# Splits in the down projections in another order: input, next sums, raw pieces; fewer fast pairs, and weight sums kept out of the output projections

## The chip, the cores and the metric

One Trainium2 chip, one core of it. The metric is the device time of one execution in microseconds (us), the median of the runs. Less is better.

## What is computed

A trunk of two encoder layers over 256 tokens of width 2048, all in float32. Each layer has an attention sub-layer (differential attention in layer 0, windowed grouped attention in layer 1, and four heads into a memory of 256 tokens), an output projection, and an MLP. The change lies in the MLP and in what is done ahead for it:

```python
for i in range(DEPTH):                       # DEPTH = 2
    h = rms_norm(x, norm_attn[i])
    ...
    x = x + heads @ w_out[i]
    h = rms_norm(x, norm_mlp[i])
    x = x + jnp.square(jax.nn.relu(h @ w_up[i])) @ w_down[i]
```

`w_up[i]` is 2048 x 8192 and `w_down[i]` 8192 x 2048, so the two MLPs hold most of the weights, and every weight is read from memory once.

## The kernel before

**Products.** A float32 product is made of three matmuls in a faster format: each operand is split into `hi`, its rounded copy, and `lo`, what the rounding left out, and hi·hi + hi·lo + lo·hi are summed (`three`, L512 to L515). `split` (L420 to L422) makes the two parts: ScalarE (ACT) casts the copy in L421, VectorE (DVE) subtracts in L422. Weights and inputs both pass through it.

**Pieces and pairs.** Weights come in pieces of 128x1024 (512 KB), in the order of `plan`. `fetch` (L361) loads and splits a piece; `piece` (L399) hands one out and keeps two more (AHEAD) fetched. Two pieces are a pair: four 128x512 blocks of weights and two of input, 24 matmuls of 128x512. An up projection has eight chunks `q` of eight pairs, a down projection two halves of 32 pairs.

**Fast pairs.** In some pairs seven block products do the work of eight (`seven`, L530): 21 matmuls in place of 24. They need sums of weight blocks: `a`, two blocks, and `b`, two more, each split like a piece (`sum_pair`, L340, with the additions of `b` in L348 and L349), and differences of the input. `load_pair` (L320) loads what the sums need, up to two pairs ahead (LOOK) if at least four of the buffers in `slots` are free. FAST, LATE, UP_FAST and OUT_FAST list the fast pairs.

**Sums made in memory.** For down projections `a` is made by the DMA queue of GpSimd (POOL) long before: `make_sums` (L283) copies a piece to `madesum` (L289), and adds blocks of the next one to it in a DMA that accumulates (L293). SUM_AT, SUM_GAP and SUM_GAP_UP say after which pieces; each copy waits for the split of a piece that has just been fetched (`after_piece`).

**Hidden blocks.** The relu and square of an up chunk (`to_hidden`, L992, on ACT in L1002 and L1003) leave 16 blocks `c` of hidden values, two pairs' input in each. Those of AWAY go to memory (`hid`, L1006) and come back (L359) into one of six `t2k` buffers, which also take half pieces of fast pairs (L333). The differences of the input of fast pairs are made once (`keep`, L977), stored (`kept`, L982) and read again when needed (L1094), all of it on POOL's queue. `h2_of` (L1050) splits the input of one pair of a down projection; it is called after both pieces of that pair are handed out, by when the next pair's are fetched.

**Order.** Each engine works through its instructions in order. A scheduler sorts them from the order of the code, by what each one needs; SP's queue issues the loads, POOL's the sums in memory, the `hid` and `kept` transfers. Buffers bound how far ahead things go: four each of raw pieces, `hi` and `lo`, eight of tag `x2` (the splits of the sums, `x` in the tables of order), six of `h2` (inputs and differences, `h`), ten of `blk`, and six slots in `big`.

Of the kernel before, what the change touches and what calls it, by code (L numbers as in the profile page):

```python
# [22 lines left out]
P = 128  # L23
S = 256
# [10 lines left out]
UP_FAST = (2, 4, 6)  # L35
# [34 lines left out]
def trunk(ctx: ExitStack, tc: tile.TileContext, xin, xtok, memin, memtok, posrel, gcol, rows,  # L70
# [167 lines left out]
    def fast_pairs(name, h):  # L238

        if name.startswith("out"):  # L240
            return OUT_FAST[h]
        if name.startswith("up"):
            return UP_FAST
        if name.startswith("down"):
            return LATE if (name, h) == ("down0", 1) else FAST
        return ()
# [16 lines left out]
    slots = deque()  # L263

# [18 lines left out]
    def make_sums(layer):  # L283

        name = f"down{layer}"

        def copy(h, j):
            made_in[name, h, j] = dp.tile([P, 2, 512], F32, name=nm("madesum"))
            after_piece(nc.gpsimd.dma_start(made_in[name, h, j].rearrange("p a n -> p (a n)"), weights[name][h, 2 * j]))  # L289

        def add(h, j):
            upper = weights[name][h, 2 * j + 1][:, 512:1024]
            nc.gpsimd.dma_start(made_in[name, h, j], upper.unsqueeze(1).broadcast_to([P, 2, 512]), accum_op=ALU.add)  # L293

        def after_piece(ins):
            tc.add_manual_dep(ins.ins, done[0].ins.name, mybir.DependencyInfo(mybir.DependencyClass.Sync, mybir.DependencyReason.DATA),
                              reason="behind a piece")
# [12 lines left out]

    making = deque()
    fetched = [0]
    before_up = [i for i, (name, c, j) in enumerate(plan) if name.startswith("up") and (c, j) == (0, 0)]
# [4 lines left out]
    loaded = {}  # L318

    def load_pair(name, c, p, early=False):  # L320
# [19 lines left out]
    def sum_pair(name, c, p):  # L340

        key = (name, c, p)
        first, raw, a, taken = loaded.pop(key)
        if a is None:
# [3 lines left out]
        nc.vector.tensor_tensor(b[:, 0, :], a[:, 1, :], first[:, 0:512], op=ALU.add)  # L348
        nc.vector.tensor_tensor(b[:, 1, :], b[:, 0, :], raw[:, 0:512], op=ALU.add)  # L349
# [4 lines left out]
        slots.extend(taken)  # L354
# [6 lines left out]
    def fetch(parts=1, lead=None):  # L361
# [6 lines left out]
        if seven_:  # L368
            load_pair(name, c, p)
            raw = loaded[name, c, p][j % 2]  # L370
        else:
            raw = wp.tile([P, 1024], F32, tag="raw", name=nm("raw"))
# [10 lines left out]
        if seven_:  # L383
            with tc.issue_after(done[0].ins):
                if j % 2 == 1:
                    split(hi[:, 0:512], lo[:, 0:512], raw[:, 0:512])
                    sum_pair(name, c, p)
                else:
                    split(hi, lo, raw)
        else:  # L390
            for i in range(parts):
# [4 lines left out]
                done[0] = split(hi[:, s], lo[:, s], raw[:, s])  # L396
        ready.append(((name, c, j), hi, lo))
# [132 lines left out]
    def seven(own, side, first_, last_, two, sums2, at, t2):  # L530
# [11 lines left out]
        three(side[2], first_, last_, d(2), (bh, bl), LOWER)  # L542
        three(own[0][1], False, False, lambda part: at(1, 1, part), (bh, bl), UPPER)
# [422 lines left out]
    def mlp(layer, X2, last):  # L966
# [4 lines left out]
        slots.extend(wide[:, i] for i in range(4))  # L971
# [38 lines left out]
        for q in range(8):  # L1010
            tag, other = ("mm", "aux") if q % 2 == 0 else ("aux", "mm")
            own = [[bank(tag) for _ in range(2)] for _ in range(2)]
            for j in range(8):
                if j == UP_FAST[0]:
                    side = [bank(other) for _ in range(4)]
                if q == 0 and j + 1 in UP_FAST:
                    diffs[j + 1] = quad("h2" if j + 1 == UP_FAST[0] else "blk", (P, 2, 512))
                    pair_differences(X2.pairs[j + 1], diffs[j + 1])
# [5 lines left out]

                if j in UP_FAST:
                    seven(own, side, j == UP_FAST[0], j == UP_FAST[-1], two, sums.pop((name, q, j)), at, diffs[j])
# [10 lines left out]
                if j == UP_FAST[-1]:  # L1037
# [7 lines left out]
        slots.extend(blk([P, 4, S], F32) for _ in range(2))  # L1045
# [9 lines left out]
        for half_ in range(2):  # L1055
# [219 lines left out]
```

## Time and profile before

| | |
|---|---|
| time, median of 3 runs | 2109.35 us (2105.58 to 2110.53) |
| the profiled execution | 2104.56 us |
| its span in the trace | 2102.8 us |
| TensorE (PE) busy | 2079.2 us, 99% |
| VectorE (DVE) busy | 1781.1 us, 85% |
| ScalarE (ACT) busy | 1278.5 us, 61% |
| read and written in memory | 532.76 MB and 94.50 MB, 298 GB/s |

In us from the span's start, the up projection of layer 0 runs from about 417 to 768, its down projection to 1105; layer 1 has them at about 1410 to 1759 and to 2102. The second halves of the down projections begin at about 950 and 1929.

A row of the timeline gives start, duration, engine, line, operation, the tiles written and read, the number of equal instructions in a row, and in brackets how long the engine stood idle before and what ended that. Durations of matmuls overlap, since they are pipelined: their starts tell the rate. A row of the windows gives the length of the stretch, PE's busy time and the number of its matmuls with a record, the granted clock, the busy share of the DMA engines and GB/s. A row of the waits reads: who, on which line, waits for whom: us in all, times, longest.

### The profile page before, as it was taken

The page shows a single profiled execution, that of the slowest core. Times are in us where ns is not written, and L with a number is a line of the kernel's source. Part 1 is how long each engine was busy: PE and PEld are TensorE (multiplying, and loading weights), DVE is VectorE, ACT ScalarE, POOL GpSimd, SP SyncE. Part 2 cuts the span into 40 slices and gives each one's busy share as a digit, 9 for nine tenths or more (in the row PEclk, how much of TensorE's full clock was granted, in tenths as well). Part 3 has the DMA queues.
Part 4 walks back from the last instruction along what each step waited for, and adds up shares of the span by engine and source line. Part 5 has one row for each costly group of instructions (what it writes and reads, how often), then busy time and mean ns, then how long its engine had stood idle before and what let it go on. Part 6 is the DMA issues. An engine that isn't in the chain of part 4 may idle for free.

```text
span 2102.8 us, 28801 instructions
## 1 busy us (share of the span) xinstructions
PE 2079.2 (99%) x9999; PEld 1719.7 (82%) x9999; DVE 1781.1 (85%) x2571; ACT 1278.5 (61%) x1902; POOL 185.1 (9%) x290
## 2 busy tenths in 40 slices
PE   9999999999999999999999999999999999999999
PEld 8888888788888888788888888888888887878877
DVE  7677778898999898898877677889999888888887
ACT  7467665565665666667555566556665656666664
POOL 1200000100010100000000100010001110000000
PEclk9999999999999999999999999999999999999999
DMA  9788877877887789978968878787888899998894
GB/s 320 262 270 262 264 239 215 255 233 235 254 296 249 251 312 307 329 259 283 326 248 262 248 226 251 216 252 230 266 262 264 282 305 320 305 330 291 298 326 151
DMA packets 168002, 565.21 MB, mean 269 GB/s; under 512 B 19424, under 2 KB 20448, under 8 KB 166624
## 3 DMA queue, kind: packets, MB, share of 16 engines
q1 hardware_dynamic: 131680, 438.05, 59.5%
q0 software_dynamic: 36032, 125.32, 22.3%
q8 instruction: 78, 1.28, 0.2%
q14 instruction: 68, 0.56, 0.1%
q10 hardware_dynamic: 144, 0.01, 0.0%
HBM read 532.76 MB, written 94.50 MB: 298 GB/s over the span
## 4 chain that ended last, share of the span: by engine, by line
PE 71%; issue 11%; DMA 9%; DVE 6%; ACT 2%; POOL 1%; SPq 0%; ACTq 0%; DVEq 0%; POOLq 0%
PE mm L515 9%; PE mm L514 9%; PE mm L513 9%; PE aux L514 8%; PE aux L515 8%; PE aux L513 8%; PE mm L474 5%; PE mm L475 5%; PE mm L476 5%; DMA madesum<-in_w_down 4%; DVE lo L422 3%; DMA big<-in_w_up 1%; DVE x L422 1%; DMA kept<-h 1%; DMA t2k<-hid 1%
## 5 line engine op out<-in xcount | busy, mean ns | idle before, releaser
L422 DVE TENSOR_TENSOR lo<-raw,hi 128x1024 fp32r<-128x1024 f32 (+1 forms) x514 | 607.7, 1206 | 175.2 <-ACT hi L421 174.1
L421 ACT CAST hi<-raw 128x1024 fp32r<-128x1024 f32 (+1 forms) x514 | 517.0, 1036 | 371.2 <-PE mm L476 119.5
L474 PE MATMUL mm<-hi,x 128*128 128x512 f32 x640 | 256.5, 403 | 1.9 <-ACT x L417 1.9
L475 PE MATMUL mm<-lo,x 128*128 128x512 f32 x640 | 251.0, 392 | 0.1
L476 PE MATMUL mm<-hi,x 128*128 128x512 f32 x640 | 250.1, 391 | 0.0
L421 ACT CAST h<-big 128x1024 fp32r<-128x1024 f32 (+1 forms) x112 | 110.3, 993 | 119.1 <-DVE big L281 93.6
L513 PE MATMUL mm<-hi,h 128*128 128x512 f32 (+1 forms) x451 | 176.5, 392 | 3.8 <-ACT h L421 3.8
L515 PE MATMUL mm<-hi,h 128*128 128x512 f32 (+1 forms) x451 | 175.5, 394 | 4.9 <-DVE h L422 4.8
L514 PE MATMUL mm<-lo,h 128*128 128x512 f32 (+1 forms) x451 | 176.6, 392 | 0.3 <-DVE lo L422 0.2
L515 PE MATMUL aux<-hi,h 128*128 128x512 f32 x444 | 172.7, 390 | 4.0 <-DVE h L422 3.9
L514 PE MATMUL aux<-lo,h 128*128 128x512 f32 x444 | 172.9, 389 | 0.7 <-DVE lo L422 0.7
L513 PE MATMUL aux<-hi,h 128*128 128x512 f32 x444 | 173.0, 390 | 0.0
L421 ACT CAST hi<-big 128x1024 fp32r<-128x1024 f32 (+1 forms) x136 | 120.3, 899 | 63.6 <-DMA big<-in_w_up 29.0
L513 PE MATMUL aux<-hi,x 128*128 128x512 f32 x400 | 156.3, 391 | 0.0
L514 PE MATMUL aux<-lo,x 128*128 128x512 f32 x400 | 155.8, 389 | 0.0
L514 PE MATMUL mm<-lo,x 128*128 128x512 f32 x400 | 155.4, 389 | 0.0
L515 PE MATMUL mm<-hi,x 128*128 128x512 f32 x400 | 155.4, 389 | 0.0
L515 PE MATMUL aux<-hi,x 128*128 128x512 f32 x400 | 155.4, 389 | 0.0
L513 PE MATMUL mm<-hi,x 128*128 128x512 f32 x400 | 155.2, 391 | 0.0
L422 DVE TENSOR_TENSOR lo<-big,hi 128x1024 fp32r<-128x1024 f32 (+1 forms) x136 | 137.8, 1031 | 13.7 <-ACT hi L421 13.5
L474 PEld LDWEIGHTS mm<-hi,x 128*128 128x128 f32 x640 | 120.6, 189 | 26.0 <-ACT x L417 2.2
L476 PEld LDWEIGHTS mm<-hi,x 128*128 128x128 f32 x640 | 120.3, 188 | 25.9
(314 smaller groups left out, 4256.2 us busy)
## 6 DMA issues: line engine op xcount, KB each, us to landing
raw<-in_w_up SPq DMA_DIRECT2D x160, 512.0 KB, 5.3
raw<-in_w_down SPq DMA_DIRECT2D x134, 512.0 KB, 4.8
madesum<-in_w_down POOLq DMA_DIRECT2D x122, 512.0 KB, 6.2
big<-in_w_up SPq DMA_DIRECT2D x96, 512.0 KB, 4.8
raw<-in_w_a SPq DMA_DIRECT2D x72, 512.0 KB, 5.3
h<-kept POOLq DMA_DIRECT2D x61, 512.0 KB, 6.3
raw<-in_w_out SPq DMA_DIRECT2D x52, 512.0 KB, 5.4
raw<-in_w_b SPq DMA_DIRECT2D x48, 512.0 KB, 5.2
```

What stands on the lines that cost most here:

```text
L421: nc.scalar.copy(hi, src)
L422: return nc.vector.tensor_tensor(lo, src, as32(hi), op=ALU.subtract)
L474: nc.tensor.matmul(ps[t], lhsT=xh, rhs=hi[:, ws], start=(k == 0), stop=False)
L475: nc.tensor.matmul(ps[t], lhsT=xh, rhs=lo[:, ws], start=False, stop=False)
L476: nc.tensor.matmul(ps[t], lhsT=xl, rhs=hi[:, ws], start=False, stop=(k == KT - 1))
L513: nc.tensor.matmul(acc_, lhsT=x(0), rhs=w2[0][:, ws], start=first_, stop=False)
L514: nc.tensor.matmul(acc_, lhsT=x(0), rhs=w2[1][:, ws], start=False, stop=False)
L515: nc.tensor.matmul(acc_, lhsT=x(1), rhs=w2[0][:, ws], start=False, stop=last_)
```

## The change

1. The lists: FAST has 15 pairs for 16, every second one and 29, where before it had neighbours (10 and 11, 15 and 16, 20 and 21); LATE, for the second half of layer 0's down projection, has 14 for 13. The first up chunk of each layer has two fast pairs for three. Pair 2 is no longer among them, and the differences for 4, 6 and 2 are made at pairs 3, 5 and 7 (DIFF_UP).
2. In a down projection the sums of a pair are made ahead of its raw pieces, and the input of pair j + 1 is split between the two pieces of pair j. Slots go back one piece later (`held_slots`).
3. In up projections `b` is written over the raw piece that it is made from, so a pair takes three slots for four; five slots are there from the start, and early loads start when two are free.
4. The copies of `make_sums` wait for the oldest of the last four splits in place of the latest. They come every fourth piece before the memory projection, every eighth from the first piece of up on, and none begins between.
5. Hidden block 14 goes away too, so only 15 of the late ones stays in `big`.

```diff
-UP_FAST = (2, 4, 6)
+UP_FAST = ((4, 6),) + ((2, 4, 6),) * 7
+DIFF_UP = {3: 4, 5: 6, 7: 2}
-FAST = (2, 4, 6, 8, 10, 11, 13, 15, 16, 18, 20, 21, 23, 25, 27, 29)
-LATE = (2, 4, 6, 8, 10, 13, 15, 18, 20, 23, 25, 27, 29)
-AWAY = range(6, 14)
-LATE_BLK = (10, 15, 20, 25, 29)
+FAST = (2, 4, 6, 8, 10, 12, 14, 16, 18, 20, 22, 24, 26, 28, 29)
+LATE = (2, 4, 6, 8, 10, 12, 14, 16, 18, 20, 22, 24, 26, 28)
+AWAY = range(6, 15)
+LATE_BLK = (8, 12, 16, 20, 24, 28)
-SUM_AT = {0: 26, 1: 2}
-SUM_GAP = 5
-SUM_GAP_UP = 10
+SUM_AT = {0: 20, 1: 2}
+SUM_GAP = 4
+SUM_GAP_UP = 8
...
         def after_piece(ins):
-            tc.add_manual_dep(ins.ins, done[0].ins.name, ...
+            tc.add_manual_dep(ins.ins, splits[0], ...
...
-        at = fetched[0] + SUM_AT[layer]
+        first, quiet, up = [at_piece[k, layer] for k in ("in", "mem", "up")]
+        at = first + SUM_AT[layer]
         for i in range(len(wanted) + 1):
             making.append((at, lambda i=i: step(i)))
-            at += SUM_GAP if at < before_up[layer] else SUM_GAP_UP
+            at += SUM_GAP if at < quiet else SUM_GAP_UP
+            at = max(at, up) if at >= quiet else at
...
+    splits = deque(maxlen=AHEAD + 2)
...
-        if key in loaded or p not in fast_pairs(name, c) or early and len(slots) < 4:
+        if key in loaded or key in taken_raw or p not in fast_pairs(name, c) or early and len(slots) < (2 if name.startswith("up") else 4):
...
-        b = raw_quad(name, (P, 2, 512), taken)
-        nc.vector.tensor_tensor(b[:, 0, :], a[:, 1, :], first[:, 0:512], op=ALU.add)
-        nc.vector.tensor_tensor(b[:, 1, :], b[:, 0, :], raw[:, 0:512], op=ALU.add)
+        b = raw.rearrange("p (a n) -> p a n", a=2) if up else raw_quad(name, (P, 2, 512), taken)
+        nc.vector.tensor_tensor(b[:, 1, :], a[:, 1, :], first[:, 0:512], op=ALU.add)
+        nc.vector.tensor_tensor(b[:, 0, :], b[:, 1, :], raw[:, 0:512], op=ALU.add)
...
             with tc.issue_after(done[0].ins):
-                if j % 2 == 1:
+                if j % 2 == 0:
+                    if down:
+                        taken = sum_pair(name, c, p)
+                    split(hi, lo, raw)
+                else:
                     split(hi[:, 0:512], lo[:, 0:512], raw[:, 0:512])
-                    sum_pair(name, c, p)
-                else:
-                    split(hi, lo, raw)
+                    if not down:
+                        taken = sum_pair(name, c, p)
+                    slots.extend(held_slots.pop(name, []) if down else taken)
+                if down and j % 2 == 0:
+                    held_slots[name] = taken
...
-            hT.append(wide[:, c - 10] if c >= 14 else blk([P, 4, S], F32))
+            hT.append(wide[:, 5] if c == 15 else blk([P, 4, S], F32))
...
+            ats = deque([h2_of(0)])
             for j in range(32):
...
-                two = [piece(f"down{layer}", half_, 2 * j + i) for i in range(2)]
-                at = h2_of(j)
+                two = [piece(f"down{layer}", half_, 2 * j)]
+                if j < 31:
+                    ats.append(h2_of(j + 1))
+                two.append(piece(f"down{layer}", half_, 2 * j + 1))
+                at = ats.popleft()
```

What the scheduler makes of it, first in the middle of layer 1's first down half. DVE before: `lo<-raw` are the raw pieces of plain pair 17, L348 to the second `x` are the sums of pair 18 with its own pieces (`lo`) between them, and the `h` are the inputs of pairs 17, 18 and 19.

```order
L422 TENSOR_TENSOR lo_17573<-raw_17569,hi_17572 128x1024
L422 TENSOR_TENSOR lo_17579<-raw_17577,hi_17578 128x1024
L348 TENSOR_TENSOR big_13687<-big_13687,blk_16803 128x512
L422 TENSOR_TENSOR x_17626<-big_13687,x_17625 128x1024
L422 TENSOR_TENSOR lo_17616<-blk_16803,hi_17615 128x1024
L422 TENSOR_TENSOR lo_17620<-t2k_17521,hi_17619 128x512
L349 TENSOR_TENSOR big_13687<-big_13687,t2k_17521 128x512
L422 TENSOR_TENSOR h_17633<-t2k_17523,h_17633 128x512
L422 TENSOR_TENSOR h_17678<-t2k_17570,h_17678 128x512
L422 TENSOR_TENSOR x_17628<-big_13687,x_17627 128x1024
L422 TENSOR_TENSOR h_17724<-t2k_17613,h_17724 128x512
```

DVE after, a little earlier in the same half (L440 is now the subtraction of `split`, L357 and L358 the sums of `b`): inputs of pairs 14 and 15, raw pieces of 13, sums and pieces of 14, inputs of 16 and 17, raw pieces of 15.

```order
L440 TENSOR_TENSOR h_17421<-t2k_17362,h_17421 128x512
L440 TENSOR_TENSOR h_17460<-t2k_17405,h_17460 128x512
L440 TENSOR_TENSOR lo_17365<-raw_17361,hi_17364 128x1024
L440 TENSOR_TENSOR lo_17374<-raw_17372,hi_17373 128x1024
L357 TENSOR_TENSOR big_13666<-big_13666 128x512
L440 TENSOR_TENSOR x_17412<-big_13666,x_17411 128x1024
L358 TENSOR_TENSOR big_13666<-big_13666,t2k_17312 128x512
L440 TENSOR_TENSOR lo_17408<-big_13666,hi_17407 128x1024
L440 TENSOR_TENSOR lo_17425<-t2k_17312,hi_17424 128x512
L440 TENSOR_TENSOR x_17414<-big_13666,x_17413 128x1024
L440 TENSOR_TENSOR h_17512<-t2k_17453,h_17512 128x512
L440 TENSOR_TENSOR h_17551<-t2k_17496,h_17551 128x512
```

A pair's input, which stood behind that pair's raw pieces and behind the sums of the next one, now stands ahead of its raw pieces, two pairs earlier; the sums stand ahead of the pieces of their own pair.

The second place is the start of layer 1's down projection. ACT before: raw pieces of pair 0, a sum of pair 2 (`x`), raw pieces of pair 1, an input for differences, the input of pair 0 (`h_16822`), and the relu and square of hidden blocks 14 and 15.

```order
L421 CAST hi_16764<-raw_16759 128x1024
L421 CAST hi_16770<-raw_16769 128x1024
L421 CAST x_16891<-big_13687 128x1024
L421 CAST hi_16811<-raw_16810 128x1024
L421 CAST hi_16817<-raw_16816 128x1024
L421 CAST h_16750<-t2k_16751 128x512
L421 CAST h_16822<-blk_14135 128x512
L1002 ACTIVATE big_13687<-aux_16849 128x512
L1002 ACTIVATE big_13687<-aux_16856 128x512
L1003 ACTIVATE big_13687<-big_13687 128x512 x2
```

ACT after, from the input of pair 0 (`h_16776`) on: raw pieces of the last up pair, the copy for the up chunk's side sums, raw pieces of pair 0, inputs of pairs 1 and 2, raw pieces of pair 1, the first piece and a sum of pair 2, then relu and square of block 14 (L1020, L1021).

```order
L439 CAST h_16776<-blk_14108 128x512
L439 CAST hi_16678<-raw_16677 128x1024
L439 CAST hi_16684<-raw_16683 128x1024
L566 COPY t2k_16710<-mm_16507 128x512
L439 CAST hi_16725<-raw_16720 128x1024
L439 CAST hi_16731<-raw_16730 128x1024
L439 CAST h_16785<-blk_14108 128x512
L439 CAST h_16869<-blk_14123 128x512
L439 CAST hi_16780<-raw_16779 128x1024
L439 CAST hi_16789<-raw_16788 128x1024
L439 CAST hi_16855<-big_13666 128x1024
L439 CAST x_16861<-big_13666 128x1024
```

The input of pair 0 moves from behind pair 1's raw pieces to ahead of the last pieces of up. PE now also runs pair 0 ahead of the transposes of blocks 14 and 15, which stood before it.

The third is POOL's queue at the same start. Before, from the last sum in memory on (L289, L293) to the first `kept` reads (L1094):

```order
L982 DMA kept_16581<-h_16574 128x1024
L289 DMA madesum_16635<-in_w_down 16x8192
L293 DMA madesum_16635<-in_w_down 256x1x512
L982 DMA kept_16757<-h_16750 128x1024
L1094 DMA h_16945<-kept_14335 128x1024
```

After (L291 and L295 make the sums, L1024 stores `hid`, L1118 reads `kept`):

```order
L1000 DMA kept_16632<-h_16625 128x1024
L291 DMA madesum_16737<-in_w_down 16x8192
L291 DMA madesum_16769<-in_w_down 16x8192
L295 DMA madesum_16737<-in_w_down 256x1x512
L295 DMA madesum_16769<-in_w_down 256x1x512
L1024 DMA hid_16826<-blk_16818 128x512
L1024 DMA hid_16835<-blk_16818 128x512
L1118 DMA h_16928<-kept_14308 128x1024
L1000 DMA kept_16907<-h_16900 128x1024
```

The first `kept` read, which came behind a `kept` store, now comes behind one more sum and the two `hid` stores of block 14. Over the whole program PE has 12 instructions more (10,066 for 10,054 rows) and DVE 26 fewer (2488 for 2514).

More of the change, by code (lines that the diff above doesn't have):

```diff
@@ L396, in fetch @@
                 done[0] = split(hi[:, s], lo[:, s], raw[:, s])
+                splits.append(done[0].ins.name)
         ready.append(((name, c, j), hi, lo))
@@ L541, in seven @@
         three(side[3], first_, last_, d(1), (ah, al), LOWER)
-        three(side[2], first_, last_, d(2), (bh, bl), LOWER)
-        three(own[0][1], False, False, lambda part: at(1, 1, part), (bh, bl), UPPER)
+        three(side[2], first_, last_, d(2), (bh, bl), UPPER)
+        three(own[0][1], False, False, lambda part: at(1, 1, part), (bh, bl), LOWER)
     def side_sums(side):
@@ L970, in mlp @@
         slots.clear()
-        slots.extend(wide[:, i] for i in range(4))
+        slots.extend(wide[:, i] for i in range(5))
         hidden_in.clear()
@@ L1023, in at @@
                     return pair[:, kk, part, t * P:(t + 1) * P]
-                if j in UP_FAST:
-                    seven(own, side, j == UP_FAST[0], j == UP_FAST[-1], two, sums.pop((name, q, j)), at, diffs[j])
+                if j in fast:
+                    seven(own, side, j == fast[0], j == fast[-1], two, sums.pop((name, q, j)), at, diffs[j])
                 elif j < 7:
@@ L1044, in mlp @@
             Task([lambda q=q, u=u, n=n, i=i, tag=tag: to_hidden(q, n, u, i, tag) for n in range(2) for i in range(2)], wait=1, gap=0)
-        slots.extend(blk([P, 4, S], F32) for _ in range(2))
+        slots.append(blk([P, 4, S], F32))
         N2 = Halves()
```

29 lines of the change are left out of this document (19 added, 10 removed).

## The prediction, made before the result was known

> **What bounds the kernel now.** I read the page's first table, then who TensorE (PE) waits for, then PE's busy time by stretches, and only then the places where it stands still.
>
> ```profile
> span 2102.8 us, 28801 instructions
> PE 2079.2 (99%) x9999; PEld 1719.7 (82%) x9999; DVE 1781.1 (85%) x2571; ACT 1278.5 (61%) x1902; POOL 185.1 (9%) x290
> ```
>
> PE is busy for 2079.2 of 2102.8 us, so 23.6 us of it are idle. All that a new order can win is this idle time and whatever PE does slowly after it. The waits of PE (us in total, times, longest):
>
> ```profile
> PE mm L515 <- DVE h L422: 4.8, 2, 2.5
> PE mm L513 <- ACT h L421: 4.0, 3, 3.2
> PE aux L515 <- DVE h L422: 3.9, 2, 2.2
> PE mm L474 <- ACT x L417: 1.9, 1, 1.9
> ```
>
> Three of the four largest name `h` in L421 or L422: the split of a pair's input in the down projections, by ACT (hi) and DVE (lo). L422's four waits come to 8.7 us. Now stretches of 50 us: busy PE and its matmuls, granted clock, DMA share, GB/s.
>
> ```profile
> 750.00:800.00 50.00, 49.41 (x226) 1.00 0.91 330
> 800.00:850.00 50.00, 49.69 (x217) 1.00 0.90 301
> 850.00:900.00 50.00, 47.47 (x203) 0.97 0.93 330
> ...
> 950.00:1000.00 50.00, 50.00 (x222) 1.00 0.81 276
> ...
> 1750.00:1800.00 50.00, 46.40 (x207) 0.97 0.96 333
> ...
> 1850.00:1900.00 50.00, 47.71 (x203) 0.97 0.88 314
> ...
> 2000.00:2050.00 50.00, 46.05 (x202) 1.00 0.92 322
> ```
>
> The undisturbed stretch at 950 sets the price of one 128x512 matmul: 50 us / 222 = 0.225 us. Against it the stretches at 800, 850, 1850 and 2000 lack 5 + 19 + 19 + 20 = 63 matmuls, 14.2 us. Their idle time alone is 0.31 + 2.53 + 2.29 + 3.95 = 9.1 us; most of the rest is slow matmuls after a stall, and some may be records the trace lost. PE at two of the stalls:
>
> ```profile
> 1853.43 1.22 PE L515 MATMUL mm<-hi,h 128*128 128x512 f32 x2 [2.27 <-DVE h L422]
> 1854.45 0.63 PE L514 MATMUL mm<-lo,h 128*128 128x512 f32 x1
> 1854.87 0.63 PE L515 MATMUL mm<-hi,h 128*128 128x512 f32 x1
> ...
> 2021.40 0.73 PE L515 MATMUL aux<-hi,h 128*128 128x512 f32 x2 [2.25 <-DVE h L422]
> 2021.98 0.39 PE L514 MATMUL aux<-lo,h 128*128 128x512 f32 x1
> ```
>
> After 2.27 us of idling the next matmuls start 0.42 us apart, at half speed, for eight of them (some 1.6 us); after 2.25 us at 2021 they run on at full speed. The Trainium skill ("TensorE: Matmul & The Clock Gate", "Why this matters for your kernels") asks for no idle gap over about 3 us; by it a gap of 2.27 us would carry no surcharge, and the trace differs: this one did. By that rule the stalls that may vanish are worth the 9.1 us, not the 14.2.
>
> Why `h` is late, on DVE before the stall at 1853:
>
> ```profile
> 1832.08 0.69 DVE L422 TENSOR_TENSOR h<-t2k,h 128x512 fp32r<-128x512 f32 x1 [4.09 <-ACT h L421]
> 1833.04 2.36 DVE L422 TENSOR_TENSOR lo<-raw,hi 128x1024 fp32r<-128x1024 f32 x2 [0.26 <-ACT hi L421]
> ...
> 1848.61 0.69 DVE L348 TENSOR_TENSOR big<-big,blk 128x512 f32<-128x512 f32 x1
> 1849.21 1.22 DVE L422 TENSOR_TENSOR x<-big,x 128x1024 fp32r<-128x1024 f32 x1
> 1850.35 1.22 DVE L422 TENSOR_TENSOR lo<-blk,hi 128x1024 fp32r<-128x1024 f32 x1
> ...
> 1852.08 0.69 DVE L349 TENSOR_TENSOR big<-big,t2k 128x512 f32<-128x512 f32 x1
> 1852.69 1.29 DVE L422 TENSOR_TENSOR h<-t2k,h 128x512 fp32r<-128x512 f32 x2
> ```
>
> DVE stands 4.09 us at 1828, and from 1833.04 works without a break until the missing `h` at 1852.69. PE waits there for the input of pair 17, a plain pair whose own two raw pieces had long been split; ahead of its input stand the sums of pair 18. The starts in these rows give a 128x1024 step at 1.13 us and a 128x512 one at 0.60. A fast pair thus costs DVE two sums (1.2), their two splits (2.3), one and a half raw pieces (1.7) and the input (0.6), 5.8 us, against 21 matmuls or 4.7 us of PE; a plain pair costs 2.9 against 24 or 5.4. Pairs 10 to 18 of FAST before hold six fast and three plain: 43.5 of DVE to 44.4 of PE. There is no slack to catch up 4.09 us.
>
> **The change part by part.**
>
> *Order and even spacing (A).* With pairs fast in turn, two pairs cost DVE 8.7 of PE's 10.1 us, so a delay is worked off at 1.4 us in each two pairs; and the inputs of pairs 14 and 15 now stand ahead of the sums of 14 and the raw pieces of 15. All four waits of L515 are of this one kind. They are worth 9.1 us (idle alone) to 14.2 (all that is lacking). I take 13, near the upper end, since slow matmuls after a stall are seen. What is late next: the raw pieces. They are due at a pair's first matmul, but can't start before PE frees their hi and lo buffers at the end of the pair before the last, which leaves the full 4.7 to 5.4 us of a pair for about 3 us of casts and subtractions.
>
> *Start of a down projection (B).* The rows are ACT's, PE's, then POOL's, and the DMA table of 765 to 790 us:
>
> ```profile
> 1758.33 1.04 ACT L421 CAST hi<-raw 128x1024 fp32r<-128x1024 f32 x1 [3.79 <-DMA raw<-in_w_down]
> ...
> 1761.07 0.61 ACT L421 CAST h<-blk 128x512 fp32r<-128x512 f32 x1
> 1761.59 1.08 ACT L1002 ACTIVATE big<-aux 128x512 f32<-128x512 f32 x2
> 1762.55 1.15 ACT L1003 ACTIVATE big<-big 128x512 f32<-128x512 f32 x2
> ```
> ```profile
> 1756.00 1.14 PE L1000 MATMUL aux<-ident,t2k 128*128 128x128 f32 x9
> 1757.55 0.98 PE L1000 MATMUL aux<-ident,t2k 128*128 128x128 f32 x7 [0.40 <-DVE t2k L990]
> 1761.73 0.80 PE L513 MATMUL mm<-hi,h 128*128 128x512 f32 x1 [3.20 <-ACT h L421]
> ```
> ```profile
> 1762.73 0.57 POOL L1094 DMA_DIRECT2D h<-kept  x1
> ```
> ```profile
> h<-kept POOLq DMA_DIRECT2D x3, 512.0 KB, 8.3
> ```
> ```profile
> h<-kept POOLq DMA_DIRECT2D x61, 512.0 KB, 6.3
> ```
>
> Before, the input of pair 0 stands on ACT behind both raw pieces of pair 1, which land late; PE waits 0.40 and 3.20 us, and the 1750 stretch holds 191 large matmuls (43.0 us) and 16 transposes (2.1): 4.9 us are lacking. In layer 0 it is at most the 0.8 us that L513's other two waits leave of their 4.0. Now that input comes early, and pair 0 runs at once, ahead of the transposes of the last hidden blocks: 5.7 us saved. But the first `kept` read, for pair 2, now stands on POOL behind two `hid` stores of hidden block 14, and those wait for its relu and square. If pair 0 starts at T, its matmuls end at T + 5.4; ACT has one cast of pair 2 and one more ahead (2 us), then L1002 and L1003 on two tiles each (2.1 us); two stores on POOL take 1.1: the read goes out near T + 10.5. At 6.3 us (median of all) to 8.3 (median of this stretch) it lands at T + 16.8 to 18.8. PE wants it after pair 0 (5.4), the transposes (2.1), pair 1 (5.4) and twelve matmuls (2.7), T + 15.6. The new stall is 1.2 to 3.2 us in each layer, with half-speed matmuls up to 4.8; the lower end is nearer to the page's median, the upper to the crowded stretch. I take 2 each, 4 in all; B is then -1.7, with bounds -3.3 and +3.9.
>
> *Output projections and the first up chunk (C).*
>
> ```profile
> 400.00:450.00 50.00, 48.21 (x215) 1.00 0.70 211
> 450.00:500.00 50.00, 49.05 (x223) 1.00 0.77 246
> ...
> 1390.00:1440.00 50.00, 49.43 (x223) 1.00 0.73 210
> ```
>
> The sum transfers leave the stretch from the memory projection to the first up chunk, pair 2 of that chunk is fast no longer, and its differences spread over three pairs. The stretches lack 1.79 + 0.57 us, and the wait of L474 above, in the second memory projection, is 1.9: 4.3 us. The bounds are 0 and 4.3; I take 3, as each has a sum transfer or pair 2's sums beside it.
>
> *Fewer fast pairs (D).* Two in down, two in up: four pairs with 24 matmuls for 21, 12 x 0.225 = +2.7 us, all on PE.
>
> *Sum transfers closer together in up (E).* They move from every tenth piece to every eighth, in step with two `kept` stores a chunk. Stretch 450 to 500, with 0.95 us idle, is what such a meeting costs: from 0 to 14 times 0.95 = 13 us for the up chunks but the first of each layer. I take 1.5, near the lower end, as one meeting in five shows in the trace so far. Block 14's `hid` stores and reloads lie on queues beside PE, at nothing, as long as DMA has room: the share is 0.96 at most.
>
> The sum: -13 - 1.7 - 3 + 2.7 + 1.5 = -13.5 us. The profiled execution takes 2104.56 us (1.8 beyond its span), so 2091.1; it lies 4.8 below the median of the runs, 2109.35, from which the forecast is **2095.9**.
>
> **Rivals.** What a measurement of this kernel can tell from no change is about 0.3%, 6.3 us.
>
> 1. *Slower: the early input waits for its reload.* For blocks 6 to 14 the input comes from memory, and in the new order it stands ahead of sums and raw pieces on ACT and DVE, so a late reload holds everything.
>
> ```profile
>   ACT h L421: 25.8, 8
> DMA to landing us min/median/max: 2.6/5.7/10.6
> ```
>
> Those are the waits for the 64 reloads before: eight, 3.2 us each. Read from SP's order after the change, the reload for pair 15 takes the buffer that the input of pair 12 leaves, one turn of two pairs, 10.1 us, before its own use. The median of 5.7 lands in time, the maximum of 10.6 doesn't. 18 pairs a half, four halves, make 36 turns; at 0.38 us a turn the 13.5 us are gone, at 0.75 us (27 us) the result is 13.5 us slower, 2122.9. Against it: each turn can work off 1.4 us.
>
> 2. *No change: the stalls move.* Half of A returns at raw pieces (-6.5), B is at +3.9, C at -1: with D and E +0.6, 2110. For it speaks the DMA share of 0.88 to 0.96 in every disturbed stretch.
>
> 3. *No change: E at its upper end.* -13.5 - 1.5 + 13 = -2, 2107. Against it: up has DVE and DMA to spare (0.77).
>
> 4. *More.* A and C whole, B at -3.3, E nothing: -14.2 - 4.3 - 3.3 + 2.7 = -19.1, 2090.2. The runs of before reach 3.8 us below their median (2105.58 to 2109.35), which puts the lower edge near 2087.
>
> That the change isn't made by the scheduler is excluded: the order shows it.
>
> **How the numbers follow.** Forecast (8 to 18 us less) 0.55, rival 4 0.12, rival 2 0.14, rival 3 0.08, rival 1 0.11. Faster by over 0.3% (below 2103.0) are the forecast, rival 4 and 0.02 of the third: 0.69. Within 0.3%: 0.20. Slower: 0.11. The range goes from rival 4's 2087 to 2110, where rivals 2 and 3 lie; outside are rival 1 and a few strays.
>
> **What would show it.** Right: no wait of L515's counterpart for `h` over 1 us; 222 matmuls in all 50-us stretches of both down projections past their first; no wait at the first matmul of down, but one for `kept` of 1 to 3 us at pair 2; 12 more matmuls; quiet out projections. Wrong: ACT's waits for `hid` above 25.8 us with PE idle behind them; PE waiting for `lo<-raw` at the heads of pairs; stalls in every up chunk beside the sum transfers; an unchanged 14 us lacking in down.

## The result, and the profile after

The changed kernel takes 2086.76 us (median of 4 runs, 2086.09 to 2087.77), the kernel before 2108.05 (its three runs and one more, 2105.58 to 2110.53). The ratio is 0.9899, with a 95% interval of 0.9882 to 0.9917: 21.3 us less. The forecast was 2095.9, and the measured median lies 0.2 us below 2087, the lower end of its range. The profiled executions are closer together: 2104.56 and 2087.19, 17.4 us apart.

The page's head, then who PE waits for, in the changed kernel:

```profile
span 2085.4 us, 28771 instructions
PE 2073.3 (99%) x10011; PEld 1721.3 (83%) x10011; DVE 1771.0 (85%) x2545; ACT 1275.6 (61%) x1892; POOL 182.8 (9%) x286
```
```profile
PE mm L531 <- DMA h<-kept: 5.0, 2, 2.6
...
PE mm L532 <- DVE lo L440: 0.8, 1, 0.8
```

PE's idle time fell from 23.6 to 12.1 us. Of the four lines shown of before none is left: PE no longer waits for an `h` that ACT or DVE splits (8.7 us in L515 and 4.0 in L513 before), nor 1.9 us in L474. The list is headed by a wait that wasn't there, for the `kept` read.

PE in the stretches shown of before, and two more (the last is of 60 us):

```profile
750.00:800.00 50.00, 47.38 (x216) 1.00 0.92 323
800.00:850.00 50.00, 50.00 (x222) 1.00 0.90 311
850.00:900.00 50.00, 50.00 (x223) 1.00 0.97 329
...
1750.00:1800.00 50.00, 46.67 (x201) 0.93 0.97 329
...
1850.00:1900.00 50.00, 50.00 (x222) 1.00 0.91 318
...
2000.00:2050.00 50.00, 50.00 (x222) 1.00 0.96 333
```
```profile
400.00:450.00 50.00, 50.00 (x230) 1.00 0.70 216
450.00:500.00 50.00, 50.00 (x231) 1.00 0.82 262
1230.00:1290.00 60.00, 59.84 (x310) 1.00 0.64 213
...
1390.00:1440.00 50.00, 50.00 (x230) 1.00 0.76 238
```

The inside of both down projections is full: 222 or 223 matmuls in each of these stretches, with a DMA share up to 0.97. Only their first stretches got worse, 216 for 226 and 201 for 207. The head of up went from 215, 223 and 223 matmuls to 230, 231 and 230.

The wait for `kept` in layer 1: POOL's two `hid` stores and the read behind them, then PE's first matmul of the down projection, and its first with that tile.

```profile
1755.24 1.16 POOL L1024 DMA_DIRECT2D hid<-blk  x2 [8.99 <-ACT blk L1021]
1756.39 0.56 POOL L1118 DMA_DIRECT2D h<-kept  x1
```
```profile
1745.23 0.39 PE L531 MATMUL mm<-hi,h 128*128 128x512 f32 x1
```
```profile
1764.58 0.79 PE L531 MATMUL mm<-hi,h 128*128 128x512 f32 x1 [2.57 <-DMA h<-kept]
1765.17 0.63 PE L532 MATMUL mm<-lo,h 128*128 128x512 f32 x1
```

The down projection starts at 1745.23 with no wait; call that moment T. POOL waits 8.99 us for the square of block 14 (L1021) and issues the read at T + 11.2; PE gets it at T + 19.3 and had stood for 2.57 us.

The reloads of hidden blocks, on which the slower rival hung: who waited, and the time to landing (those of L368 alone, without the `hid` stores).

```profile
  ACT h L439: 1.3, 3
...
DMA to landing us min/median/max: 3.4/5.5/11.1
```

Three waits and 1.3 us for 72 reloads, where before it was eight and 25.8 us for 64, though the slowest took longer than before (11.1 us for 7.7).

### The profile page after: what moved, and what is told of

Same layout as the page of the kernel before. It is cut to its first block, busy times and chain, and to the rows that moved or that the text cites. A ratio compares the mean times of both kernels' runs of the same rounds, so it can differ in the third digit from the quotient of the medians.

```text
span 2085.4 us, 28771 instructions
## 1 busy us (share of the span) xinstructions
PE 2073.3 (99%) x10011; PEld 1721.3 (83%) x10011; DVE 1771.0 (85%) x2545; ACT 1275.6 (61%) x1892; POOL 182.8 (9%) x286
## 4 chain that ended last, share of the span: by engine, by line
PE 95%; DMA 2%; DVE 1%; issue 1%; ACT 1%; POOL 0%; SPq 0%; ACTq 0%; DVEq 0%; POOLq 0%
PE mm L531 12%; PE mm L532 12%; PE mm L533 12%; PE aux L532 11%; PE aux L533 11%; PE aux L531 11%; PE mm L492 7%; PE mm L493 7%; PE mm L494 7%; DMA h<-kept 1%; PE mm L1018 1%; PE aux L635 1%; DVE lo L440 1%; PE aux L612 1%; PE aux L654 1%
## 5 line engine op out<-in xcount | busy, mean ns | idle before, releaser
L439 ACT CAST hi<-raw 128x1024 fp32r<-128x1024 f32 (+1 forms) x522 | 525.4, 1036 | 451.1 <-issue 143.4
L440 DVE TENSOR_TENSOR lo<-raw,hi 128x1024 fp32r<-128x1024 f32 (+1 forms) x522 | 617.4, 1207 | 196.1 <-ACT hi L439 194.1
L492 PE MATMUL mm<-hi,x 128*128 128x512 f32 x640 | 256.0, 402 | 0.2 <-ACT hi L439 0.2
L493 PE MATMUL mm<-lo,x 128*128 128x512 f32 x640 | 251.0, 392 | 0.2 <-DVE lo L440 0.2
L494 PE MATMUL mm<-hi,x 128*128 128x512 f32 x640 | 250.3, 391 | 0.2 <-DVE x L436 0.2
L439 ACT CAST h<-big 128x1024 fp32r<-128x1024 f32 (+1 forms) x100 | 101.7, 1020 | 151.6 <-DVE big L283 129.6
L531 PE MATMUL mm<-hi,h 128*128 128x512 f32 (+1 forms) x461 | 179.8, 390 | 5.2 <-DMA h<-kept 5.0
L533 PE MATMUL mm<-hi,h 128*128 128x512 f32 (+1 forms) x461 | 178.9, 388 | 0.0
L531 PE MATMUL mm<-hi,x 128*128 128x512 f32 x414 | 161.8, 391 | 0.0
L533 PE MATMUL mm<-hi,x 128*128 128x512 f32 x414 | 161.1, 389 | 0.0
L532 PE MATMUL mm<-lo,x 128*128 128x512 f32 x414 | 161.1, 389 | 0.0
L440 DVE TENSOR_TENSOR lo<-big,hi 128x1024 fp32r<-128x1024 f32 (+1 forms) x141 | 144.4, 1044 | 0.2 <-ACT hi L439 0.2
L493 PEld LDWEIGHTS mm<-lo,x 128*128 128x128 f32 x640 | 120.5, 188 | 23.7 <-DVE lo L440 1.8
```

The lines of the kernel that those rows point to most:

```text
L439: nc.scalar.copy(hi, src)
L440: return nc.vector.tensor_tensor(lo, src, as32(hi), op=ALU.subtract)
L492: nc.tensor.matmul(ps[t], lhsT=xh, rhs=hi[:, ws], start=(k == 0), stop=False)
L493: nc.tensor.matmul(ps[t], lhsT=xh, rhs=lo[:, ws], start=False, stop=False)
L494: nc.tensor.matmul(ps[t], lhsT=xl, rhs=hi[:, ws], start=False, stop=(k == KT - 1))
L531: nc.tensor.matmul(acc_, lhsT=x(0), rhs=w2[0][:, ws], start=first_, stop=False)
```

## The experiments

Ratios are to the kernel before, run on the same chip in the same job. There were four jobs, each on a chip of its own; the kernel before took 2104.2, 2104.4, 2103.7 and 2102.7 us in them, single runs from 2098.7 to 2113.3. So times of two jobs can be compared by their ratios only, and the changed kernel itself ran in the second job alone.

### Which part of the reorder removed the waits for h

First the new lists with the old order of splits in the down projections. The edit undoes both moves:

```diff
                 if j % 2 == 0:
-                    if down:
-                        taken = sum_pair(name, c, p)
                     split(hi, lo, raw)
                 else:
                     split(hi[:, 0:512], lo[:, 0:512], raw[:, 0:512])
-                    ...
+                    slots.extend(sum_pair(name, c, p))
...
-                two = [piece(f"down{layer}", half_, 2 * j)]
-                ...
-                at = ats.popleft()
+                two = [piece(f"down{layer}", half_, 2 * j + i) for i in range(2)]
+                at = h2_of(j)
```

> The changed kernel with the old order of splits in the down projections (raw pieces, then sums, then the input of a pair after both its pieces); lists of fast pairs and times of the sums in memory stay new. Changed kernel: 2086.8 us. Theory 'order': PE's waits for h in L515's place return, 8 to 14 us: 2095 to 2101. Rival 'even spacing': with every second pair fast DVE works a delay off, no wait for h over 1 us: 2085 to 2090.

Measured: 2094.70 us, ratio 0.9948 (0.9930 to 0.9965). The time is about that of theory 'order', but not its reason. PE's largest wait, and ACT's in layer 0's second half (950 to 1105 us):

```profile
PE aux L526 <- DVE lo L434: 5.2, 12, 0.8
```
```profile
ACT blk L433 <- DMA big<-madesum: 18.2, 4, 5.1
```

No wait for `h` came back. Instead PE waits twelve times for `lo`, all in that half, while ACT stands 18.2 us for sums that have not been loaded into `big` (and some more for those in `blk`). Two rows of ACT's timeline there show what is queued behind such a sum:

```profile
1001.16 1.05 ACT L433 CAST blk<-blk 128x1024 fp32r<-128x1024 f32 x1 [5.04 <-DMA blk<-madesum]
1002.12 1.99 ACT L433 CAST hi<-raw 128x1024 fp32r<-128x1024 f32 x2
```

The raw pieces of a plain pair wait behind a late load for the sums of the next fast one. The three stretches from 950 to 1100 lack 42 matmuls against the changed kernel, 9.5 us; the four that lacked 63 before are full (222 each). So the rival was right about `h`, and a wait took its place that neither had named.

Then the new lists alone, in the kernel before:

```diff
-FAST = (2, 4, 6, 8, 10, 11, 13, 15, 16, 18, 20, 21, 23, 25, 27, 29)
-LATE = (2, 4, 6, 8, 10, 13, 15, 18, 20, 23, 25, 27, 29)
+FAST = (2, 4, 6, 8, 10, 12, 14, 16, 18, 20, 22, 24, 26, 28, 29)
+LATE = (2, 4, 6, 8, 10, 12, 14, 16, 18, 20, 22, 24, 26, 28)
...
-LATE_BLK = (10, 15, 20, 25, 29)
+LATE_BLK = (8, 12, 16, 20, 24, 28)
```

> The kernel before with the new lists of fast pairs of the down projections alone (FAST, LATE and where the sums' splits of LATE go). Two fast pairs fewer are +1.4 us. Theory 'order': the four waits of L515 for h stay (8.7 us of waiting), 2107 to 2111. Rival 'even spacing': the waits go, 14 us less: 2094 to 2097.

Measured: 2105.84 us, ratio 1.0004 (0.9990 to 1.0019).

```profile
PE aux L514 <- DVE lo L422: 5.0, 12, 0.8
PE mm L513 <- DMA h<-kept: 2.5, 2, 1.5
PE mm L515 <- DVE h L422: 2.1, 2, 1.1
```
```profile
850.00:900.00 50.00, 50.00 (x222) 1.00 0.95 327
1000.00:1050.00 50.00, 48.48 (x208) 1.00 0.87 313
1850.00:1900.00 50.00, 50.00 (x223) 1.00 0.93 321
2000.00:2050.00 50.00, 50.00 (x222) 1.00 0.97 333
```

The time is nearest to theory 'order', the rows are the rival's once more: L515's waits for `h` fell from 8.7 to 2.1 us, the two left are at the starts of the down projections, and the stretches that lacked 63 matmuls are full with the old order too. Waits for `lo` took their place (5.0 us, ten of the twelve in layer 0's second half, where 35 matmuls are lacking that before were there, 7.9 us), with `kept` on top and, as two pairs fewer are fast, six more matmuls. A time alone would have confirmed the wrong theory here.

Next, one move undone at a time, the lists new. The input late, the sums still early (the second half of the first diff):

> The changed kernel with the input of pair j split after both pieces of pair j again (the sums stay ahead of the raw pieces). With raw pieces and input both in the old place the run 'old order' took 0.9948 of the kernel before, against 0.9899, and PE waited for lo twelve times in layer 0's second half. Theory: those waits come from sums that give their slots back late and so load madesum late, which the early sums cure; then the late input costs at most 2 us: ratio 0.989 to 0.9915. Rival: the early input is the cure: ratio 0.993 to 0.996 with the twelve waits for lo.

Measured: 2091.33 us, ratio 0.9935 (0.9914 to 0.9957). The twelve waits are gone, as 'slots' said, but the late input costs more than the 2 us that it allowed:

```profile
PE mm L531 <- DMA h<-kept: 6.9, 2, 3.6
PE aux L531 <- DMA h<-kept: 2.4, 2, 1.7
```

All of it lies at the starts of the down projections (9.3 us for `kept`, where the changed kernel has 5.0, and 1.7 for an `h`). The sums late, the input still early (the first half of that diff):

> The changed kernel with the sums of a fast pair made after its raw pieces in the down projections again, slots given back with them (the input stays early). Theory 'slots': the twelve waits of PE for lo in layer 0's second half return, behind ACT's waits of 5 us for madesum: ratio 0.993 to 0.996. Rival 'early input is the cure': ratio 0.989 to 0.9915, no such waits.

Measured: 2091.22 us, ratio 0.9934 (0.9913 to 0.9955).

```profile
PE mm L525 <- DMA h<-kept: 4.2, 2, 2.4
PE aux L526 <- DVE lo L434: 2.5, 7, 0.8
```

Seven of the twelve waits returned, half their time, and with them ACT's for `madesum` in layer 0's second half (11.4 us for `big` and 7.0 for `blk`; the changed kernel has none there). The changed kernel beside these two:

> The changed kernel as it is, beside the others on the same chip: ratio 0.988 to 0.992, the first fast pair of both down projections waiting 2.5 us for kept.

Measured: 2086.93 us, ratio 0.9913 (0.9880 to 0.9945), 2084.04 to 2088.73. Its runs all lie below those of the late input (2089.66 to 2094.60) and of the late sums (2089.07 to 2093.73). Each move is worth about 4.4 us alone, and both undone cost some 7 (0.9948 for 0.9913). The early input keeps the start of a down projection short. With the early sums the next `madesum` is there in time; that this is because their slots come back earlier is argued, since that run moves the sums and the return of the slots together.

### Whether the order makes the lists unnecessary

The changed kernel with the old lists (FAST, LATE, LATE_BLK; the diff of the lists above, read backwards):

> The changed kernel with the old lists of fast pairs in the down projections (neighbours 10 and 11, 15 and 16, 20 and 21). The changed kernel: ratio 0.9899 and 0.9913. Theory 'both': order alone doesn't make room for two fast pairs in a row, waits for lo or h of 5 to 14 us come back near 860, 1850 and 2020: ratio 0.993 to 0.998. Rival 'order suffices': no such waits, and two fast pairs more save 1.35 us: ratio 0.989 to 0.991.

Measured: 2116.73 us, ratio 1.0053 (1.0038 to 1.0068), slower than before and outside both expectations.

```profile
PE mm L531 <- DMA h<-kept: 19.1, 2, 16.8
```
```profile
1772.06 1.12 POOL L295 DMA_DIRECT2D madesum<-in_w_down  x1 [13.93 <-DMA madesum<-in_w_down]
...
1773.20 1.12 POOL L1118 DMA_DIRECT2D h<-kept  x1
```

Most of it is one wait of 16.8 us that neither theory had. With 32 fast pairs the sums of layer 1 don't fit into up any more; four are left over at its end, and POOL stands 13.93 us for the copy of the last one, with the `hid` store and the `kept` read behind it. To take that away, the old lists again, the sums every seventh piece in up, and two early `kept` reads (both edits are shown below):

> The changed kernel with the old lists of fast pairs, the sums in memory every seventh piece in up in place of every eighth, and the first two kept reads of a down projection early. Theory 'neighbours lose in any order': the waits for lo (2.4 and 1.9 us, with slow matmuls 8 us in the rows) stay, ratio 0.991 to 0.996. Rival 'it was the queue alone': two fast pairs more save 1.35 us, ratio 0.987 to 0.990.

Measured: 2108.54 us, ratio 1.0014 (0.9992 to 1.0037), above both expectations, single runs from 2098.83 to 2114.63. PE in the profiled execution, one of the quicker at 2100.51:

```profile
PE mm L531 <- ACT h L439: 8.0, 2, 4.3
PE mm L532 <- DVE lo L440: 4.8, 8, 2.5
```
```profile
850.00:900.00 50.00, 48.18 (x207) 1.00 0.94 329
1850.00:1900.00 50.00, 49.50 (x217) 1.00 0.93 332
2000.00:2050.00 50.00, 49.29 (x216) 1.00 0.97 334
```

The stretches that lacked 58 matmuls before lack 15 + 5 + 6 = 26, 5.9 us, now mostly for `lo`. The order mends more than half of them, not all. Most of the rest is at the starts, where with these lists the input of pair 0 came late again (8.0 us). Why single runs reach 2114 is open; the longest have a granted clock of 0.995 where the profiled one has 0.998, and no trace shows behind which stalls it fell.

### The sums in memory

The changed kernel with the old times:

```diff
-SUM_AT = {0: 20, 1: 2}
-SUM_GAP = 4
-SUM_GAP_UP = 8
+SUM_AT = {0: 26, 1: 2}
+SUM_GAP = 5
+SUM_GAP_UP = 10
...
-            tc.add_manual_dep(ins.ins, splits[0], ...
+            tc.add_manual_dep(ins.ins, done[0].ins.name, ...
...
-            at += SUM_GAP if at < quiet else SUM_GAP_UP
-            at = max(at, up) if at >= quiet else at
+            at += SUM_GAP if at < up else SUM_GAP_UP
```

> The changed kernel with the old times of the sums in memory (every fifth piece from the 26th, every tenth in up, none left out between, each behind the latest split). Theory: the sum transfers made the idle time around the output projections and in up, 7 to 10 us by the two traces: 2093 to 2097, with DMA share back to 0.7 to 0.8 in the stretches from 1290 on and stalls beside madesum. Rival: the first up chunk's new fast pairs and the smaller slots did it: 2086 to 2089.

Measured: 2093.39 us, ratio 0.9940 (0.9921 to 0.9960).

```profile
400.00:450.00 50.00, 48.63 (x221) 1.00 0.72 219
450.00:500.00 50.00, 48.34 (x220) 1.00 0.73 227
1230.00:1290.00 60.00, 58.03 (x293) 0.97 0.78 232
1390.00:1440.00 50.00, 49.85 (x229) 1.00 0.77 228
```

Against the changed kernel 9 + 11 + 17 + 1 matmuls are missing in these stretches, some 8 us. The theory holds, but for the stretch from 1390: it stayed nearly full with the old times, so there another part of the change (the first up chunk's list or its slots) is enough. The other way round, the new times alone in the kernel before (the same diff, read backwards):

> The kernel before with the new times of the sums in memory alone. In the changed kernel the old times cost 6 to 9 us. Theory: the gain is the same without the rest, idle and slow time between 400 and 450, at 1271 and 1395 goes: ratio 0.995 to 0.9975. Rival: it needs the new slots and lists, or the closer transfers cost as much in up: ratio 0.998 to 1.001.

Measured: 2115.41 us, ratio 1.0058 (1.0037 to 1.0079), above both expectations; the profiled execution is the longest of the seven, 2121.08.

```profile
PE mm L519 <- DMA h<-kept: 12.1, 1, 12.1
```
```profile
400.00:450.00 50.00, 50.00 (x228) 1.00 0.71 211
640.00:690.00 50.00, 47.53 (x217) 1.00 0.89 293
```

The gain at the head of up is there without the rest (the next stretch holds 230, and that from 1390 228). It is more than eaten by sums left over at the end of up, as with the old lists (12.1 us), and by waits inside up (2.5 us idle between 640 and 690): the closer transfers do cost there, where the kernel before and the changed one both have 50.00 us of PE busy. Which of its other parts spares the changed kernel this was not tried.

### The first kept read

The changed kernel with that read ahead of the last up chunk's tasks:

```diff
+            if q == 7:
+                early = quad("h2", (P, 2, 512))
+                nc.gpsimd.dma_start(early, kept[FAST[0]])
             Task([lambda q=q, u=u, n=n, i=i, tag=tag: to_hidden ...
...
```

> The changed kernel with the kept read for the first fast pair of a down projection issued ahead of the last up chunk's hid stores on POOL's queue. Theory 'queue place': the waits for kept (2.48 and 2.57 us, with slow matmuls after the second some 8 us in the start-to-start rows) go: 2079 to 2082. Rival 'crowded DMA': the read lands as late, or another load of that stretch is late in its place: 2085 to 2088.

Measured: 2084.11 us, ratio 0.9898 (0.9882 to 0.9913).

```profile
PE mm L531 <- DMA h<-kept: 2.8, 2, 1.7
PE mm L532 <- DVE lo L440: 1.9, 2, 1.3
```

About half of each theory by the rows: the first read's wait is gone, the second read stands behind two `kept` stores. By its ratio the run can't be told from the changed kernel (0.9899 and 0.9913). With both early:

```diff
+            if q == 7:
+                early = [quad("h2", (P, 2, 512))]
+                nc.gpsimd.dma_start(early[0], kept[FAST[0]])
...
+            if half_ == 0:
+                early.append(quad("h2", (P, 2, 512)))
+                nc.gpsimd.dma_start(early[1], kept[fast[1]])
             ats = deque([h2_of(0)])
...
```

> The changed kernel with the kept reads for the first two fast pairs of a down projection issued ahead of the last up chunk's stores on POOL's queue. With one of them early, the second read still waited behind two kept stores and cost 1.66 and 1.18 us on PE. Theory 'queue place': no wait for kept is left, 3 to 8 us below the changed kernel on this chip. Rival 'crowded DMA': other loads of that stretch are late in its place (lo in the first fast pairs), at most 3 us below.

Measured: 2082.58 us, ratio 0.9892 (0.9864 to 0.9920), 4.4 below the changed kernel in the same job, though their single runs overlap (2079.30 to 2085.12, and 2084.04 to 2088.73). No wait for `kept` is left. The rival has its part too:

```profile
PE mm L532 <- DVE lo L440: 3.7, 2, 2.2
```

Is it the two sums left over in layer 1? This edit of the changed kernel leaves none:

```diff
-SUM_GAP_UP = 8
+SUM_GAP_UP = 7
```

> The changed kernel with the sums in memory every seventh piece in up, so that none is left over at its end (two were, in layer 1). Theory 'leftover sums': the wait for kept in layer 1 (2.57 us) shrinks, that of layer 0 (2.48 us, where none was left over) stays: 0 to 3 us below the changed kernel, ratio 0.988 to 0.991. Rival 'the hid stores alone set it': both stay as they are, ratio 0.990 to 0.992; stalls in up from the closer transfers would show there.

Measured: 2086.02 us, ratio 0.9913 (0.9888 to 0.9938).

```profile
PE mm L531 <- DMA h<-kept: 5.6, 2, 3.2
```

They don't matter: the wait in layer 1 is 3.2 us without them, and POOL's queue there holds only the two `hid` stores ahead of the read, as in layer 0.

### The first up chunk, and the best of all

The changed kernel with pair 2 fast there too:

```diff
-UP_FAST = ((4, 6),) + ((2, 4, 6),) * 7
-DIFF_UP = {3: 4, 5: 6, 7: 2}
+UP_FAST = ((2, 4, 6),) * 8
+DIFF_UP = {1: 2, 3: 4, 5: 6}
```

> The changed kernel with three fast pairs in the first up chunk again (pair 2 too, differences at pairs 1, 3 and 5). Six matmuls fewer are 1.35 us. Theory: pair 2's sums crowd DVE at the head of up, 1 to 3 us of waits near 440 and 1430, so within 2 us of the changed kernel: ratio 0.9895 to 0.9915. Rival: the waits there came from the sum transfers alone, no waits: ratio 0.9885 to 0.9905.

Measured: 2088.82 us, ratio 0.9921 (0.9893 to 0.9950). No wait at the head of up, but no gain that could be measured either. The same beside two early reads:

> The changed kernel with two early kept reads and three fast pairs in the first up chunk. With two early reads alone: ratio 0.9892 beside 0.9913 of the changed kernel. Theory: the six matmuls come on top, ratio 0.988 to 0.9895. Rival: waits at the head of up eat them: 0.989 to 0.991.

Measured: 2081.67 us, ratio 0.9898 (0.9863 to 0.9932), not to be told from the 0.9892 without it. Both with SUM_GAP_UP at 7:

> Two early kept reads, three fast pairs in the first up chunk, sums in memory every seventh piece in up. With the first two: ratio 0.9898 (median 2081.67 us, the lowest so far). Theory: with no sums at the end of up the loads of the first pairs land earlier and the wait for lo there (1.83 and 1.46 us) shrinks: 1 to 3 us less. Rival: it comes from the two last kept stores that hold the buffers: no change within 1 us.

Measured: 2079.49 us (2079.20 to 2080.49), ratio 0.9883 (0.9854 to 0.9912), the lowest of all, though by the intervals not to be told from the two runs before it.

The two waits for `lo` didn't shrink (3.4 us, where they were 3.7 and 3.3 with two early reads), so the rival is right about them. The profiled executions, 2079.38 and 2081.26 with SUM_GAP_UP at 8, differ in the granted clock: the longer one has a spell of half clock from 787.65 to 791.07 behind such a wait, which costs 1.7 us, and the shorter has none up to its last microseconds.

## Why the prediction was right or wrong

**What bounded it** was right: PE, through single stalls, most of them for the input in the down projections. Every sign that the prediction named for being right was seen; what failed are sizes.

**A**, forecast -13: the stretches from 800, 850, 1850 and 2000 that lacked 14.2 us lack nothing. The size was right. The reason was half of it: the prediction put order and spacing into one term. The spacing alone fills all four stretches, but brings waits for `lo` in layer 0's second half (7.9 us), and the kernel is no faster for it; the new order takes these away. The order without the lists leaves 26 of the 63 lacking, mostly for `lo`; that two fast pairs in a row are too dense for DVE fits the prediction's sum (43.5 of DVE to 44.4 of PE), but no run tried it by itself.

**B**, forecast -1.7 within -3.3 and +3.9: the two first stretches lack 10 + 6 = 16 more matmuls, +3.6 us. The mechanism came as written, in both layers. The read went out at T + 11.2 for 10.5 and landed at T + 19.3 for 16.8 to 18.8; the waits were 2.48 and 2.57 us for 2 each. Mis-sized was what follows a wait: in layer 1 `lo` was 0.76 us late just ahead of it, and PE ran at half the clock for 6.80 us behind it, which costs 3.4 us where the upper bound allowed 1.6. So B came out near that bound, not at -1.7.

**C and E are the step that failed, by how they were costed.** C was bounded at 4.3 us by adding up idle time in two stretches and one wait, and taken at -3; E was put at +1.5, from the idle time between 450 and 500. The matmul counts, which A had used, show 15 + 8 + 7 more in these three stretches, 6.8 us, and the memory projection another 1.8 (59.84 us busy for 58.05). Together that is -8.5 where the forecast had -1.5. Idle time is the wrong measure for such short stalls: at 400.77 PE had been idle for 0.67 us, but that matmul started 0.83 us later than at the full rate and the next one another 0.10. And the transfers in up didn't multiply the stall at 450; it went away. The runs give size and cause again: the old times of the sums cost some 8 us, and the new times alone fill these stretches.

**D**, +2.7, stands as a count, twelve matmuls more in PE's order; its price was not measured, since the six matmuls fewer of the first up chunk showed no gain.

With these sizes the sum is -14.2 + 3.6 - 8.5 + 2.7 = -16.4, against the 17.4 us between the profiled executions; the last 1.0 us is not accounted for. Had C been counted like A, the range would have reached to near 2083.

**The base.** The forecast was set off from a median of three runs, 2109.35, that a fourth moved to 2108.05. The medians are 21.3 us apart, the profiled executions 17.4: the profiled execution of before is quicker than all its four runs, and the prediction added those 4.8 us to the changed kernel too, whose profiled execution lies 0.4 above its median. Of the 9.1 us by which the forecast was too high, 5.2 come from this step and 3.9 from the terms.

**Rivals.** The early input didn't wait for its reload (1.3 us): the lead of one turn, 10.1 us, was enough for all but three of 72. The 5.7 and 10.6 us on which that rival was built are of reloads and `hid` stores together; the reloads alone took 2.6 to 7.7 us before, less than the lead. What the rival described, a late load holding raw pieces on ACT, does exist: it is ACT's wait for `madesum` in the old order. The stalls did move in part, to `kept`. The dense sums did cost in up when they came alone (2.5 us idle from 640 on), not in the changed kernel.

## What to carry to other kernels

Cost a term in matmuls lacking per stretch, not in idle time alone: half of what a stall costs can lie beside the wait that is shown. When a wait goes, look at what stands next in the same queue: here the new lists alone (1.0004), the new times alone (1.0058) and the new order and times without the lists (1.0053, and 1.0014 with two early reads) gained nothing, since each turned one wait into another, and together they paid. In a queue that issues transfers in order, what must wait (a store behind an activation, a sum behind its copy) belongs behind the read that the next stage needs.

## What the runs showed of the hardware that was not expected

A stall doesn't slow PE by its length alone. Gaps of 2.25 us (before, at 2021) and 2.48 us (after, at 781) were followed by matmuls at full rate, 0.23 us apart; gaps of 2.27 us (before, at 1853) and 2.57 us (after, at 1764) by ones 0.42 us apart, eight and a dozen of them. The gap of 2.48 us, then PE behind that of 2.27 us in rows of one microsecond, where the granted clock is 0.50:

```profile
781.03 0.51 PE L531 MATMUL mm<-hi,h 128*128 128x512 f32 x1 [2.48 <-DMA h<-kept]
```
```profile
1853.00:1854.00 1.00, 0.57 (x1) 0.66 1.15 381
1854.00:1855.00 1.00, 1.00 (x4) 0.50 0.98 356
...
1856.00:1857.00 1.00, 1.00 (x4) 0.63 0.97 387
```

Read at their shares, such rows put the half clock at 860.05 to 863.46, 1761.17 to 1764.58 and 1853.33 to 1856.74 before, three spells of 3.41 us whose starts lie 264 and 27 times 3.41 us apart, and at 1763.20 to 1770.00 after, twice 3.41 us. In the traces of the other runs too the spells are one, two, four or five times that long, but for those that the program's end cuts off. So the clock is set at steps of 3.41 us. What counts is PE's idle time within one step: with these steps laid over the 15 traces that have a spell inside the program, from 100 to 2070 us, the full clock fell at the end of every step with 1.86 us of idling or more, never with 1.70 or less, and once in three times between. The gap of 2.48 us was cut by the end of a step, with 1.60 us in the first part; 2.17 us of the gap of 2.27 us lay in one step, and 1.94 us of the 2.57 us gap and the 0.76 us wait ahead of it. In two executions of the changed kernel the clock fell at 1763.20 and 1762.39 us, which are not whole steps apart: the steps don't begin with the program.

The Trainium skill ("TensorE: Matmul & The Clock Gate", "Part 1: The HAM clock gate") says that the clock follows a window that runs freely and doesn't start with the kernel; its window of about 3.4 us agrees with the 3.41 us here, and that it is longer than all four gaps shows that not the whole of it has to be idle.

The DMAs that add up the sums in memory took up to 22.9 us to land, with a median of 7.6 (the copies ahead of them up to 14.9, median 5.9), and with the old lists one POOL instruction that waits for such a copy held everything behind it for 13.9 us. The changed kernel's adding DMAs (L295):

```profile
DMA to landing us min/median/max: 6.0/7.6/22.9
```
